# Loads of an overflow branch on GpSimd's queue in place of ScalarE's, with a larger descriptor scratch and one buffer for small values

## The chip, the cores and the metric

The kernel runs on one core of one Trainium2 chip. The core has TensorE (PE: matrix products and transposes), VectorE (DVE), ScalarE (ACT) and GpSimd (POOL) for elementwise work, SyncE (SP), which here only issues transfers, and 16 DMA engines that move data between HBM and the on-chip memory. Each engine works through its own list of instructions; they meet at semaphores. The metric is the device time of one execution in microseconds.

## The reference

The reference computes two layers on 256 tokens of width 1024, and a final RMSNorm. A layer has a mixer with three parallel groups of heads, and a hierarchical mixture of experts. All is float32. The part that matters here, shortened:

```python
def hier_moe(h, w_group, b_group, w_expert, b_expert, w_gate, w_up, w_down):
    t = h.reshape(B * S, D)                      # 256 x 1024
    g_prob = softmax(t @ w_group + b_group)      # 4 groups
    p_sel, g_idx = top_k(g_prob, 1)
    e_in = logits of the 8 experts of that group
    w_k, i_k = top_k(softmax(e_in), 2)           # 2 of 8, weights normalised
    combine = p_sel * one_hot(g_idx) * inner     # 256 x 4 x 8
    for g in range(4):
        a, b = t @ w_gate[g], t @ w_up[g]        # 8 experts of 1024 x 256
        hid = silu(a) * b * combine[:, g]
        y += hid @ w_down[g]                     # 8 experts of 256 x 1024
```

All 32 experts of a layer are read, 3 MB each, so a layer has about 100 MB of expert weights.

## The kernel before

**Staging.** Weights come from HBM into a ring of 25 slots of 1 MB each (128 partitions x 2048 floats), which also holds most intermediate values. A rehearsal of the program notes when each slot is free; from it the place of each load in SyncE's list is set. All weight loads (line 80) go through SyncE's queue, in the order in which they are used. They count on eight semaphores in turn, DMAHW0 to DMAHW7, and a load waits for the load eight before it, so that at most eight are under way. Where a slot was in use, the load also waits for the engine that used it last.

**A layer.** The mixers come first (lines 413 to 637), then the routing (640), then the experts (799). Four experts form a group; there are eight groups. For each expert at most 32 tokens (CAP) are gathered into slots by a matrix product with a 0/1 matrix (`collect`). `hidden` multiplies them with 8 MB of gate and up weights per group, `bend` and `turn` apply the gate and transpose, and for groups 0 to 3 `whole` multiplies with 4 MB of down weights and adds to x. For groups 4 to 7 the down products are put off into four rounds at the end (line 901), between which the input projection of the next layer is done.

**The overflow branch.** If an expert has more than 32 tokens, the surplus is dropped by the gathering and must be added. After group 1 the largest count of a layer is put into `flag` (line 893). After group 3, `overflow` (line 940) has each of the five engines read the flag (line 951) and compare it (line 952). The branch takes five slots of the ring, which it shares with the weights:

```python
        count = nc.values_load(flag[0:1, 0:1], min_val=0, max_val=S)
        with self.tc.If(count > CAP):
            ...
            with self.tc.For_i(0, 96, 12) as e0:
                for j in range(4):
                    for k in range(8):
                        nc.scalar.dma_start((g0, g1)[k // 4][:, k % 4 * 512:k % 4 * 512 + 512],
```

The body computes the surplus for all experts, one expert at a time, with 12 loads of 256 KB for each. In the kernel before they are issued by ScalarE's queue, which counts on the same eight semaphores as SyncE's loads. When an engine doesn't take the branch, it runs a short block in which the semaphores that the body would have raised are raised by as much; in the profile this block has line 952.

**Small values.** Values of a few bytes per partition (`ss`, `s`, `r1`, `rr`, `low`, `sums`, `cm`, `flag`, `ws` and the like) lie in the pool `sm`, where a name has two buffers by default. The names of `route` ask for one buffer themselves. SCRATCH, 512 bytes per partition, is set aside for transfer descriptors that GpSimd writes.

Of the kernel before, what the change touches and what calls it, by code (L numbers as in the profile page):

```python
# [9 lines left out]
F32 = mybir.dt.float32  # L10
# [13 lines left out]
AHEAD = 3  # L24
NV = 61
TAIL = 4
SCRATCH = 512
SM_UK, SM_UV, SM_PW, SM_RT = 0, 512, 1024, 1280


# [87 lines left out]
def v3(t, a, b, c0=0):  # L118
    return t[:, c0:c0 + a * b].rearrange("p (a b) -> p a b", a=a)


class Net:
    def __init__(self, tc, ctx, a, plan):
        self.tc, self.nc, self.a, self.plan = tc, tc.nc, a, plan
        nc = self.nc
        into = ctx.enter_context if plan else lambda c: c
        big = into(tc.tile_pool(name="big", bufs=1))
        cst = into(tc.tile_pool(name="cst", bufs=1))
        self.sm = into(tc.tile_pool(name="sm", bufs=2))
        psp = into(tc.tile_pool(name="ps", bufs=1, space=bass.MemoryType.PSUM))  # L130
        into(tc.manual_schedule())
        self.ps = psp.tile([128, 8, 512], F32, name="ps")
# [57 lines left out]
        g = nc.gpsimd  # L190
# [12 lines left out]
        for i, n in ((0, 4), (8, 32)):  # L203
            k = min(i, 4)
# [18 lines left out]
    def mm(self, out, lhsT, rhs, start, stop):  # L223
        self.nc.tensor.matmul(out, lhsT, rhs, start=start, stop=stop, skip_group_check=True)  # L224
# [574 lines left out]
    def experts(self, l, routed):  # L799
        nc, ps, ring, vec, sm, mm = self.nc, self.ps, self.ring, self.vec, self.sm, self.mm  # L800
        V, A, G = nc.vector, nc.scalar, nc.gpsimd
        r2, comb, pos, sel, st = routed
# [23 lines left out]

        def bend(g, dT):

            d, h, ws = st[g][0], st[g][2][:, 0:256], sm.tile([128, 1], F32, name="ws")
            A.activation(h, ps[:, 2, 0:256], AF.Silu)  # L830
            for t in range(2):
                self.tr(ps[:, 3, 256 + t * 128:256 + t * 128 + 128], d[:, t])
            V.tensor_reduce(ws, ps[:, 3, 256:512], axis=AX.X, op=OP.add)  # L833
            V.scalar_tensor_tensor(h, h, ws, ps[:, 2, 256:512], op0=OP.mult, op1=OP.mult)  # L834
            V.tensor_scalar(dT, ps[:, 3, 256:512], 0.0, None, op0=OP.is_gt)  # L835
# [31 lines left out]
        for g in range(8):  # L867
            if g == 8 - TAIL:
                th, tw = ring.take("th"), ring.take("tail", F32R)
            hidden(g)  # L870
            i = (g - 8 + TAIL) * 512
            hT, dT = (st[g][1][:, j:j + 2].rearrange("p k s -> p (k s)") for j in (0, 2)) if i < 0 else (
                th[:, i // 2:i // 2 + 256], tw[:, i // 2:i // 2 + 256])
            bend(g, dT)
            if g == 0:
                hv = v3(ring.take("hn"), 2, D)
                for t in range(2):
                    self.ev("a", hv[:, t], self.x[:, t], r2[:, t:t + 1])
            if g + 1 < 8:
                collect(g + 1)  # L880
            turn(g, hT)
            if i < 0:
                whole(g, hT, dT)
            else:
                tail[g] = hT, dT
                ring.drop(f"g{g}")
            if g == 1:

                cm, flag = sm.tile([128, 1], F32, name="cm"), sm.tile([128, 1], I32, name="flag")
                for t in range(2):  # L890
                    mm(ps[:, 3, 0:32], self.ones, sel[:, t], t == 0, t == 1)
                V.tensor_reduce(cm, ps[:, 3, 0:32], axis=AX.X, op=OP.max)
                V.tensor_copy(flag, cm)
            if g == 3:
                self.overflow(l, hv, comb, pos, flag)
# [44 lines left out]
    def overflow(self, l, hv, comb, pos, flag):  # L940

        nc, ps, ring, mm = self.nc, self.ps, self.ring, self.mm
        V, A, we = nc.vector, nc.scalar, self.a["we"]
        names = ("ohT", "og0", "og1", "od", "om")
        hT, g0, g1, dn, om = (ring.take(n) for n in names)
        if not self.plan:
            return ring.drop(*names)
        hx, cw = v3(hT, 8, 256), v3(om, 2, 32)
        wd = dn.rearrange("p (q c n) -> p q c n", q=4, c=2)
        hd, fT, tmp = v3(om, 2, 256, 64), v3(om, 2, 256, 576), v3(om, 2, 32, 1088)  # L950
        count = nc.values_load(flag[0:1, 0:1], min_val=0, max_val=S)
        with self.tc.If(count > CAP):
            V.tensor_scalar(cw, pos, CAP - 0.5, None, op0=OP.is_ge)
            V.tensor_tensor(cw, cw, comb, op=OP.mult)
            for k in range(8):
                for t in range(2):
                    self.tr(ps[:, k % 2, t * 128:t * 128 + 128], hv[:, t, k * 128:k * 128 + 128])
                self.ev("av"[k % 2], hx[:, k], ps[:, k % 2, 0:256], self.vec[:, l, 8 + k:9 + k])
            with self.tc.For_i(0, 96, 12) as e0:
                for j in range(4):  # L960
                    for k in range(8):
                        nc.scalar.dma_start((g0, g1)[k // 4][:, k % 4 * 512:k % 4 * 512 + 512],
                                            we[bass.ds(e0 + (l * 96 + k), 1), :, j * 512:j * 512 + 512]
                                            .rearrange("o p c -> (o p) c"))
                    for q in range(4):
                        nc.scalar.dma_start(dn[:, q * 512:q * 512 + 512],
                                          we[bass.ds(e0 + (l * 96 + 8 + q), 1), :, j * 512:j * 512 + 512]
                                          .rearrange("o p c -> (o p) c"))
                    for t in range(2):
                        for k in range(8):  # L970
                            mm(ps[:, t], hx[:, k, t * 128:t * 128 + 128], v3((g0, g1)[k // 4], 4, 512)[:, k % 4],
                               k == 0, k == 7)
                        A.activation(hd[:, t], ps[:, t, 0:256], AF.Silu)
                        V.scalar_tensor_tensor(hd[:, t], hd[:, t], cw[:, t, j:j + 1], ps[:, t, 256:512],
                                               op0=OP.mult, op1=OP.mult)
                        for c in range(2):
                            self.tr(ps[:, 3, c * 256 + t * 128:c * 256 + t * 128 + 128],
                                    hd[:, t, c * 128:c * 128 + 128])
                    V.tensor_copy(fT, v3(ps[:, 3], 2, 256))
                    for t in range(2):  # L980
                        for n in range(2):
                            for c in range(2):
                                mm(ps[:, 4 + 2 * t + n], fT[:, c, t * 128:t * 128 + 128],
                                   wd[:, 2 * n:2 * n + 2, c], c == 0, c == 1)
                            xs = self.x[:, t, n * 512:n * 512 + 512]
                            V.tensor_tensor(xs, xs, ps[:, 4 + 2 * t + n], op=OP.add)
                V.tensor_copy(tmp[:, :, 0:28], cw[:, :, 4:32])
                V.tensor_copy(cw[:, :, 0:28], tmp[:, :, 0:28])
        ring.drop(*names)
# [112 lines left out]
```

## Time and profile before

| | |
|---|---|
| median of 3 runs | 608.64 us (606.15 to 609.34) |
| the profiled execution | 607.07 us |
| its span, first to last instruction | 605.4 us |
| mean granted TensorE clock | 0.951 |
| PE busy | 530.0 us (88%) |
| DVE busy | 261.3 us (43%) |
| ACT busy | 142.4 us (24%) |
| POOL busy | 96.5 us (16%) |
| transferred | 228.67 MB, mean 378 GB/s |
| loads on SyncE's queue | 92.6% of the DMA engines' time |

Busy shares are averages over stages with different limits: TensorE is busy for most of the span, and so are the DMA engines. Which of them ends a stage is read from the waits in that stage. The page's rate row divides the span into 40 slices of 15.1 us. In it the experts of layer 0 run from about slice 9 to slice 22 and those of layer 1 from about slice 29 to the end; between them lies the mixer of layer 1. The names are those of the program: `slot` is a slot of the ring, `in_we` the expert weights, `ps` the accumulators. An engine's name with a q (SPq, POOLq) is its sequencer, where branches, semaphores and transfer issues run.

### The profile page before, as it was taken

How to read it: one execution, taken by the hardware profiler on the slowest of the kernel's cores; microseconds unless marked ns; L12 is line 12 of the kernel's file. 1: busy time of each engine (PE TensorE's matmuls, PEld its weight loads, DVE VectorE, ACT ScalarE, POOL GpSimd, SP SyncE). 2: the span in 40 equal slices, each digit the busy share in tenths (PEclk: the TensorE clock that was granted, in tenths of full speed). 3: DMA queues.
4: the chain of work that ended last, by engine and by line, in shares of the span. 5: the costliest groups of instructions: out<-in, count | busy, mean ns of one | idle time of the engine just before them, and what ended most of it. 6: DMA issues, size and time to landing. Idle time of an engine off the chain costs nothing. (4 is left out here: it accounts for less than half of the span.)

```text
span 605.4 us, 10375 instructions
## 1 busy us (share of the span) xinstructions
PE 530.0 (88%) x4168; PEld 335.9 (55%) x4168; DVE 261.3 (43%) x644; ACT 142.4 (24%) x339; POOL 96.5 (16%) x138
## 2 busy tenths in 40 slices
PE   8989999898898687779989899998898878886993
PEld 8959877554344143426768787765344425431662
DVE  5879765332333122115357876652333322221242
ACT  4476453200000000013234854322000000001222
POOL 2544322000000000002113442310000000000011
PEclk9999999999999799859999999998999997996897
DMA  8999878999999979999999959689999998999993
GB/s 309 399 421 397 331 254 326 368 391 424 421 420 420 416 292 422 423 418 419 421 420 422 422 206 333 261 334 395 422 420 421 420 419 368 372 421 422 422 410 107
DMA packets 34618, 228.67 MB, mean 378 GB/s; under 512 B 3841, under 2 KB 6145, under 8 KB 7938
## 3 DMA queue, kind: packets, MB, share of 16 engines
q1 hardware_dynamic: 34130, 227.33, 92.6%
q8 instruction: 36, 0.59, 0.4%
q10 hardware_dynamic: 432, 0.59, 0.3%
q14 instruction: 20, 0.16, 0.1%
HBM read 226.85 MB, written 1.05 MB: 376 GB/s over the span
## 5 line engine op out<-in xcount | busy, mean ns | idle before, releaser
L224 PE MATMUL ps<-slot,slot 128*32 128x256 f32 (+6 forms) x3372 | 410.1, 440 | 56.5 <-DVE slot L780 23.2
L224 PEld LDWEIGHTS ps<-slot,slot 128*32 128x32 f32 (+2 forms) x3372 | 245.6, 144 | 190.2 <-issue 91.7
L242 POOL TENSOR_TENSOR slot<-slot,slot 128x512 fp32r<-128x512 f32 (+1 forms) x38 | 50.9, 1339 | 131.0 <-DVE slot L290 53.0
L288 ACT ACTIVATE slot<-ps 128x256 fp32r<-128x256 f32 (+5 forms) x70 | 33.1, 473 | 142.8 <-PE ps L224 129.0
L833 DVE TENSOR_REDUCE ws<-ps 128x1 f32<-128x256 f32 x16 | 6.8, 424 | 133.1 <-PE ps L282 133.1
L224 PE MATMUL ps<-slot 128*128 128x256 f32 (+3 forms) x224 | 59.2, 408 | 0.0
L830 ACT ACTIVATE slot<-ps 128x256 f32<-128x256 f32 x16 | 6.1, 383 | 215.8 <-PE ps L224 215.8
L809 POOL TENSOR_TENSOR slot<-slot,comb 128x128 f32<-128x128 f32 x32 | 12.1, 399 | 270.0 <-PE ps L224 215.9
L242 DVE TENSOR_TENSOR slot<-slot,slot 128x512 fp32r<-128x512 f32 (+1 forms) x54 | 47.5, 881 | 13.5 <-ACT slot L288 13.1
L224 PEld LDWEIGHTS ps<-slot 128*128 128x128 f32 (+1 forms) x224 | 30.5, 195 | 30.9 <-issue 14.4
L793 DVE TENSOR_TENSOR slot<-ps,vec 128x512 f32<-128x512 f32 x32 | 22.1, 691 | 52.5 <-PE ps L224 52.3
L290 DVE COPY slot<-ps 128x512 f32<-128x512 f32 (+3 forms) x30 | 20.5, 689 | 40.9 <-PE ps L224 32.6
L242 DVE TENSOR_TENSOR slot<-ps,slot 128x256 fp32r<-128x256 f32 (+1 forms) x42 | 18.3, 435 | 43.8 <-ACT slot L288 43.7
L288 ACT ACTIVATE slot<-slot 128x512 fp32r<-128x512 f32 (+1 forms) x54 | 33.0, 613 | 15.4 <-PE ps L224 10.9
L282 PE MATMUL ps<-ident,slot 128*128 128x128 f32 x128 | 24.3, 295 | 5.0 <-DVE slot L835 2.9
L282 PEld LDWEIGHTS ps<-ident,slot 128*128 128x128 f32 x128 | 14.8, 145 | 24.3 <-issue 15.4
L863 DVE TENSOR_TENSOR x<-x,ps 128x512 f32<-128x512 f32 x32 | 22.0, 688 | 8.5 <-PE ps L224 8.2
L224 PE MATMUL ps<-ident,ones 128*128 128x128 f32 x108 | 19.2, 314 | 1.5 <-POOL ident L193 1.5
L244 DVE SCALAR_TENSOR_TENSOR slot<-ps,vec,slot 128x256 fp32r<-128x256 f32 x26 | 12.4, 482 | 17.8 <-ACT slot L288 17.7
L288 ACT ACTIVATE slot<-ps,vec 128x256 fp32r<-128x256 f32 x26 | 12.1, 473 | 27.6 <-PE ps L282 13.2
L290 DVE CAST slot<-slot 128x512 fp32r<-128x512 f32 (+1 forms) x38 | 18.5, 487 | 0.0
L224 PEld LDWEIGHTS ps<-ident,ones 128*128 128x128 f32 x108 | 16.1, 218 | 3.9 <-issue 2.4
(126 smaller groups left out, 303.2 us busy)
## 6 DMA issues: line engine op xcount, KB each, us to landing
slot<-in_we SPq DMA_DIRECT2D x191, 1024.0 KB, 19.2
slot<-in_wo SPq DMA_DIRECT2D x8, 1024.0 KB, 19.2
slot<-in_wvu SPq DMA_DIRECT2D x4, 1024.0 KB, 19.8
slot<-in_wqk SPq DMA_DIRECT2D x3, 1024.0 KB, 19.3
slot<-in_wa SPq DMA_DIRECT2D x3, 832.0 KB, 14.1
slot<-in_uq SPq DMA_DIRECT2D x2, 1024.0 KB, 15.5
slot<-in_small SPq DMA_DIRECT2D x2, 784.0 KB, 15.7
x<-in_x SPq DMA_DIRECT2D x4, 256.0 KB, 5.8
```

The lines of the kernel that those rows point to most:

```text
L224: self.nc.tensor.matmul(out, lhsT, rhs, start=start, stop=stop, skip_group_check=True)
L242: V.tensor_tensor(lo, in_, hi.bitcast(F32), op=OP.subtract)
L244: V.scalar_tensor_tensor(lo, in_, scale, hi.bitcast(F32), op0=OP.mult, op1=OP.subtract)
L282: self.nc.tensor.transpose(out, in_, self.ident)
L288: nc.scalar.activation(out, in_, AF.Copy, scale=1.0 if scale is None else scale)
L290: nc.vector.tensor_copy(out, in_)
L793: self.nc.vector.tensor_tensor(xs[:, 4 * n:4 * n + 4], v3(self.ps[:, b0 + n], 4, 128), self.vec[:, l, 8 + 4 * n:12 + 4 * n, None].to_broad ...
L809: G.tensor_tensor(d4, d4, comb[:, t, 4 * g:4 * g + 4, None].to_broadcast([128, 4, 32]), op=OP.mult)
L830: A.activation(h, ps[:, 2, 0:256], AF.Silu)
L833: V.tensor_reduce(ws, ps[:, 3, 256:512], axis=AX.X, op=OP.add)
L863: V.tensor_tensor(xs, xs, ps[:, 6 + n], op=OP.add)
```

## The change

The twelve loads in the body of the branch are issued by GpSimd in place of ScalarE. GpSimd's loads count on eight semaphores of their own, DMASW0 to DMASW7. The scratch for descriptors goes from 512 to 1,024 bytes. The pool `sm` has one buffer per name, and only `ws` keeps two.

```diff
-SCRATCH = 512
+SCRATCH = 1024
...
-        self.sm = into(tc.tile_pool(name="sm", bufs=2))
+        self.sm = into(tc.tile_pool(name="sm", bufs=1))
...
-            d, h, ws = st[g][0], st[g][2][:, 0:256], sm.tile([128, 1], F32, name="ws")
+            d, h, ws = st[g][0], st[g][2][:, 0:256], sm.tile([128, 1], F32, name="ws", bufs=2)
...
-                        nc.scalar.dma_start((g0, g1)[k // 4][:, k % 4 * 512:k % 4 * 512 + 512],
+                        nc.gpsimd.dma_start((g0, g1)[k // 4][:, k % 4 * 512:k % 4 * 512 + 512],
                                             we[bass.ds(e0 + (l * 96 + k), 1), :, j * 512:j * 512 + 512]
...
-                        nc.scalar.dma_start(dn[:, q * 512:q * 512 + 512],
+                        nc.gpsimd.dma_start(dn[:, q * 512:q * 512 + 512],
```

On SyncE, at the end of the branch in layer 0, the program before has the following. The row of line 952 stands for the block of the branch that isn't taken, with what it waits for; the rows of line 80 are the first weight loads behind it, by the slot that they fill.

```order
L952 UNCONDITIONAL_BRANCH [waits DMAHW0_49,DMAHW1_49,DMAHW2_49,DMAHW3_49,DMAHW4_49,DMAHW5_49,DMAHW6_49,DMAHW7_49]
L80 DMA slot_1895<-in_we 128x2048 [waits DVE_49,DMAHW1_49,PE_49,Activation_49]
L80 DMA slot_1897<-in_we 128x2048 [waits DMAHW6_49,DMAHW5_49,DMAHW7_49,DMAHW2_49,DMAHW0_49]
L80 DMA slot_1899<-in_we 128x2048 [waits DMAHW4_49,DMAHW3_49]
L80 DMA slot_1907<-in_we 128x2048 [waits PE_49]
L80 DMA slot_1913<-in_we 128x2048 [waits DMAHW5_49,PE_49]
```

The changed program has the following at the same place.

```order
L952 UNCONDITIONAL_BRANCH
L80 DMA slot_1895<-in_we 128x2048 [waits DVE_49,DMAHW1_49,PE_49,Activation_49]
L80 DMA slot_1897<-in_we 128x2048 [waits DMASW7_49,DMASW6_49,DMAHW2_49,DMASW5_49,DMASW4_49]
L80 DMA slot_1899<-in_we 128x2048 [waits DMASW3_49,DMASW2_49,DMAHW3_49,DMASW1_49,DMASW0_49]
L80 DMA slot_1907<-in_we 128x2048 [waits DMAHW4_49,PE_49]
L80 DMA slot_1913<-in_we 128x2048 [waits DMAHW5_49,PE_49]
```

The eight waits of line 952 are gone from SyncE, and the second and third load wait for semaphores of GpSimd's transfers.

On GpSimd, at the end of the same branch, the difference between the two programs is this; lines 959 are the end of the loop in the body, line 952 the block of the branch not taken, and line 809 the weighting of group 5's gathering matrix.

```order
 L959 REGISTER_ALU
 L959 COMPARE_AND_BRANCH
 L959 UNCONDITIONAL_BRANCH
+L952 ISA
 L952 UNCONDITIONAL_BRANCH
 L809 TENSOR_TENSOR slot_1956<-slot_1956,comb 128x128 x2
```

GpSimd has one more instruction in the block not taken, which raises DMASW0 to DMASW7. The body of the loop ahead of it holds the loads that stood on ScalarE before. TensorE's, VectorE's and SyncE's rows are otherwise the same.

## Rows read from the trace of the kernel before

**Rows 1.** The page, rate of transfers in 40 slices of the span
```profile
GB/s 309 399 421 397 331 254 326 368 391 424 421 420 420 416 292 422 423 418 419 421 420 422 422 206 333 261 334 395 422 420 421 420 419 368 372 421 422 422 410 107
```

**Rows 2.** The chain that ended last, layer 1's experts: start us, us, what
```profile
518.22 14.32 DMA slot<-in_we
...
532.60 20.54 DMA slot<-in_we
...
557.87 38.33 PE ps L224 x384
```

**Rows 3.** Waits of SyncE's queue, whole span: us, times, longest us
```profile
SPq L80 <- DMA slot<-in_we: 195.1, 97, 3.0
...
SPq L952 <- SPq L952: 37.2, 6, 18.5
```

**Rows 4.** Line 952: durations in ns, then first and last start us
```profile
L952 SPq EVENT_SEMAPHORE  x16: 17/17/17, 220.1 to 514.6; - x16
L952 POOLq COMPARE_BRANCH  x2: 45/45/45, 190.1 to 483.9; - x2
...
L952 SPq COMPARE_BRANCH  x2: 45/49/53, 201.6 to 495.6; - x2
```

**Rows 5.** Timeline, load issues of SyncE around both branches: start us, us
```profile
178.00 22.69 SPq L80 DMA_DIRECT2D slot<-in_we  x10
...
221.17 7.13 SPq L80 DMA_DIRECT2D slot<-in_we  x9
...
227.98 0.33 SPq L80 DMA_DIRECT2D slot<-in_we  x1
...
494.61 0.33 SPq L80 DMA_DIRECT2D slot<-in_we  x1
...
514.79 5.74 SPq L80 DMA_DIRECT2D slot<-in_we  x9
...
520.20 0.33 SPq L80 DMA_DIRECT2D slot<-in_we  x1
```

**Rows 6.** Windows: busy us of each engine, then PEclk, DMA share, GB/s
```profile
180.00:195.00 15.00, 12.47 (x138) 7.21 (x130) 4.01 (x9) 0.98 (x2) 0.76 (x2) 1.00 1.01 419
217.50:227.50 10.00, 9.17 (x83) 3.73 (x81) 2.33 (x5) 0.38 (x1) 0.76 (x2) 1.00 0.63 220
510.00:517.50 7.50, 7.50 (x60) 4.82 (x63) 1.81 (x3) 0.00 (x0) 0.76 (x2) 0.83 0.59 214
```

**Rows 7.** Timeline, TensorE behind the branch of layer 0 (idle before, releaser)
```profile
204.44 8.73 PE L224 MATMUL ps<-slot,slot 128*32 128x512 f32 x57 [4.73 <-issue]
```

**Rows 8.** TensorE's waits from 228 to 300 us, and its timeline there
```profile
PE ps L224 <- DMA slot<-in_we: 7.2, 8, 1.4
...
237.85 1.06 PE L224 MATMUL ps<-slot,slot 128*32 128x512 f32 x8 [0.21 <-DMA slot<-in_we]
...
277.61 0.64 PE L224 MATMUL ps<-slot,slot 128*32 128x256 f32 x8 [0.26 <-DMA slot<-in_we]
```

**Rows 9.** Layer 1's end: TensorE's waits (540 to 556), timeline, windows
```profile
PE ps L224 <- DMA slot<-in_we: 5.3, 5, 1.5
...
553.18 1.94 PE L224 MATMUL ps<-slot,slot 128*32 128x512 f32 x8 [0.55 <-DMA slot<-in_we]
...
593.64 1.07 PE L224 MATMUL ps<-slot,slot 128*32 128x256 f32 x16
...
550.00:555.00 5.00, 3.75 (x16) 0.40 (x16) 0.00 (x0) 0.00 (x0) 0.00 (x0) 0.50 1.01 419
590.00:592.50 2.50, 2.50 (x36) 1.42 (x26) 0.73 (x2) 0.39 (x1) 0.00 (x0) 1.00 0.79 254
592.50:595.00 2.50, 2.50 (x31) 1.76 (x28) 0.42 (x1) 0.60 (x2) 0.00 (x0) 1.00 0.02 8
```

**Rows 10.** GpSimd: the instruction's kind at the start, and behind the branch
```profile
L1095 POOLq INC_SWDGE_SEM  x1: 27/27/27, 0.2 to 0.2; - x1
...
218.94 0.76 POOL L809 TENSOR_TENSOR slot<-slot,comb 128x128 f32<-128x128 f32 x2 [28.83 <-PE ps L224]
```

## The prediction, made before the changed kernel had run

> **What bounds the kernel now.** I read the page's rate row first: the transfers run at about 420 GB/s through both expert stages, and in each stage there is one hole, where the rate falls to 292 and then to 368 and 372 [rows 1]. So there the weight stream is the resource to look at, and the question is what opens the two holes. The chain of waits comes next: from 518 to 553 us it is almost all weight transfer, and from 557.87 us it is TensorE without another transfer in it [rows 2]. The expert stage of layer 1 therefore ends when its weights land, and the tail behind it follows at TensorE's own pace. Third, the waits of SyncE's queue. Most of them are the normal ones, a load waiting for the load eight before it (195.1 us over 97 waits), but 37.2 us sit on line 952, the overflow branch, one of them 18.5 us long [rows 3]. The rows of that line show what it is: SyncE compares and branches at 201.6 and 495.6 us, and then runs 16 semaphore instructions, 8 per branch, of which the first ends at 220.1 and the last at 514.6 us [rows 4]. The overflow body itself never runs: its loads, line 962, have no row in the trace.
>
> Why SyncE waits there can be read in the program. The scalar engine's loads of the overflow body count on the same eight semaphores (DMAHW0 to 7) as SyncE's weight loads. A branch that isn't taken has to bring these semaphores to where the body would have left them, and SyncE does it: for each it waits until all earlier loads on it have landed, then adds. SyncE thus lets the weight queue run empty at each of the two branches.
>
> **What an emptied queue costs.** Before the first branch ten loads are issued in 22.69 us, 0.33 us of which is the last issue itself: (22.69 - 0.33) / 9 = 2.484 us a load of 1 MB [rows 5]. The last of them goes out at 200.36 us. After the drain nine loads are issued from 221.17 on, and the ninth, at 227.98 us, is the first that again waits for a landing [rows 5]. Nine loads at the old pace would have brought it at 200.36 + 9 x 2.484 = 222.72 us. The drain of layer 0 cost 5.26 us. The same in layer 1: 494.61 + 22.36 = 516.97 against 520.20 us, 3.23 us [rows 5]. By bytes, as a second way: from 217.5 to 227.5 us 220 GB/s were moved where 419 had been usual, (419 - 220) x 10 / 419 = 4.75 us; from 510 to 517.5 us 214, which is 3.67 us [rows 6]. The two ways sum to 8.49 and 8.42 us; I take 8.45, with 7.98 (4.75 + 3.23) and 8.93 (5.26 + 3.67) as ends.
>
> **The change part by part.**
>
> The loads of the body go to GpSimd's queue, and so to semaphores of their own (DMASW0 to 7). In the order of the changed kernel SyncE's branch row has no waits any more, and GpSimd has one instruction and the waits on its own semaphores instead. The first load behind the branch waits for the landing that any load waits for, and for TensorE, VectorE and ScalarE to have passed the branch. It would be due at 200.36 + 2.48 = 202.84 us. SyncE is through the comparison at 201.7 us [rows 4], so it issues on time. Its slots are free: the first three held down-projection weights of group 3, which TensorE is done with before its own branch, and the next ones gate and up weights of group 4; of these TensorE needs 57 multiplications in 8.73 us from 204.44 us on, 8 to a weight [rows 7], so it frees one every 1.2 us, twice as fast as loads come. So both holes close: minus 8.45 us on the transfers' side.
>
> How much of it reaches the end. Layer 0: TensorE begins to starve at 237.85 us and has its last wait for a weight, of 0.26 us, at 277.61 us [rows 8]; behind that it is bound by itself until the mixers are through. The arrival at 277.61 moves with the loads. Can TensorE be there 5.26 us earlier? It loses 7.2 us in 8 waits on the way [rows 8], more than 5.26, so it would still have some 2 us of waiting left: the loads stay the later ones, and the whole 5.26 (or 4.75) passes on. Layer 1 then runs the same course, only earlier. There the last gate and up weight is waited for at 553.18 us, and 5.3 us in 5 waits in all [rows 9], again more than the loads gain; the chain from there is TensorE's, and the 3.23 to 3.67 us pass on too. The last weights land near 592.3 us (254 GB/s until 592.5, 8 after), and are used at 593.64 [rows 9], so the tail has 1.3 us of room and isn't caught by them, since both move alike.
>
> What GpSimd pays. It now runs an instruction that raises the eight semaphores at the branch not taken. Its kind is in the trace once, at the start, with 27 ns [rows 10]; below it isn't worth anything, and above I bound it by the longest stop that an engine shows behind this branch, TensorE's 4.73 us [rows 7]. I take 27 ns. Either way it is hidden: GpSimd takes its branch at 190.1 us [rows 4] and sits idle for 28.83 us before its next work, at 218.94 [rows 10]. Without that cover each microsecond would delay the weighting of group 5. SyncE's second load waits for these semaphores too; it is due at 205.3 us, 15 us after.
>
> TensorE stands still for 4.73 us behind its branch and "issue" is all that the profile names [rows 7]. The Trainium skill (Runtime: NRT & Kernel Launch, Instruction fetch mechanics) says that a taken branch to code outside the fetched window waits until that code has been fetched. By this rule SyncE, whose wait at the branch has so far covered such a fetch, may be held likewise: 201.7 + 4.73 = 206.4 us for its next load, two loads late with six still under way, so the sum stays, but the rule gives rival 3 its chance. No row of SyncE can show it before the change.
>
> ScalarE loses the 96 loads of the two bodies and as many address instructions, none of which ran: 0. The scratch is touched by no instruction that runs: 0. One buffer for small values makes a second layer's value wait for the first's readers; the nearest case is the flag, read for layer 0 before SyncE's comparison at 201.6 us [rows 4] and written again only in the experts of layer 1, behind a whole mixer: 0. A few later instructions wait for more semaphores than before, all raised at the branch; each costs some 17 ns [rows 4], under 0.3 us in all.
>
> **The sum.** 607.07 us of the profiled execution (605.4 span and 1.7 around it) minus 8.45 is 598.6. That execution is 1.6 us below the median of the runs, from which the same sum gives 600.2. I predict the middle, 599.4 us.
>
> **The rivals.**
>
> 1. The clock gives more. From 550 to 555 us the granted clock is 0.50, the lower of the two levels (1.2 GHz), and a step of 8 multiplications takes 1.94 us instead of 1.06 [rows 8, 9], behind the waits for weights. With fewer starved loads this may not come. TensorE could then gain some 2 us until 560, but the last weights allow only the 1.3 us of room: 598.1 us. Against it: starving doesn't vanish, it only begins later, and the same fall could come elsewhere, for as much the other way.
>
> 2. Only one hole pays, or a hole is worth less. If TensorE turned out to be the later one at 277.61, where it waits only 0.26 us, layer 0's gain would be lost and 3.45 us remain: 604.4 us. Against it stand the 7.2 us of waits before. Beside it, the Trainium skill (DMA: Bandwidth & Descriptors, Anatomy of one DMA) gives a transfer from GpSimd's path a fixed cost of about 2.0 us whatever its size. Were that all that an emptied queue loses, two would be 4.0 us and the time 603.9; the trace disagrees, with 4.75 and 3.67 us.
>
> 3. It doesn't do what it says: SyncE is held behind the branch until the queue is empty all the same, by a fetch or by another engine's semaphore. It would have to be held for 18 us, and the longest stop seen is 4.73 [rows 7]. Time 607.9 us.
>
> 4. Slower: the semaphores that SyncE's second load waits for are now raised by GpSimd. They decide once GpSimd raises them later than that load goes out now, after 221.7 us, 31.6 us after its branch; from there each microsecond costs one, in both layers. At 34 us that is about 2 x 2.4, some 613 us. For it: the instruction isn't timed in this use. Against it: 27 ns in the one use that there is [rows 10].
>
> **Chances.** The forecast 0.74, with a range of its own of 597 to 602 us (the ends of the sum, 0.95 us apart, the 1.6 us between median and profiled run, and some 2 us of clock either way); rival 1 0.12; rival 2 0.07; rival 3 0.04; rival 4 0.03. A range of 595.5 to 604.0 holds the forecast, rival 1 and part of rival 2. Half a percent, 3 us, is about what a measurement of this kernel tells from no change. Faster by more: 0.92 (the forecast, rival 1 and most of rival 2); within: 0.05; slower: 0.03.
>
> **What would show it.** Right: line 952 has no long wait on SyncE, and loads follow at about 2.48 us across 200 and 490 us; the rate row has no hole in either expert stage; TensorE's starving starts some 5 us later than 237.85 or is shorter by as much; layer 1's flag read comes about 5 us earlier and the end about 8. A stop of SyncE behind the branch with the transfers still at 419 GB/s would bear out the fetch, at no cost. Wrong: a hole of the same depth with a wait on GpSimd's semaphores (rival 4) or with none (rival 3); or closed holes and a TensorE that reaches 277 us no earlier (rival 2).

## The result, and the profile after

The changed kernel takes 602.16 us (median, 601.02 to 603.37), the kernel before 608.94: 6.8 us less, a ratio of 0.9898 with an interval of 0.9867 to 0.993. Forecast were 599.4 us with a range of 595.5 to 604.0. The profiled execution took 601.43 us (span 599.8). The mechanism is the one foretold, and the gain is smaller than its sum of 8.45 us: the time lies inside the wide range, and just above the range of 597 to 602 us that the forecast had for itself.

The rate row of the page after, against [rows 1]:

```profile
GB/s 300 402 419 413 294 281 306 368 389 423 420 420 422 414 422 422 418 423 417 422 419 421 412 200 325 273 325 392 415 423 421 419 419 421 419 422 423 420 398 89
```

Both holes are gone: slice 15 stands at 422, where 292 was, slices 34 and 35 at 421 and 419, where 368 and 372 were. The windows that had 220 and 214 GB/s [rows 6] now read (last column GB/s, before it PEclk and DMA share):

```profile
217.50:227.50 10.00, 9.82 (x88) 4.38 (x87) 1.86 (x4) 0.38 (x1) 0.76 (x2) 1.00 1.02 420
510.00:517.50 7.50, 7.38 (x67) 2.11 (x66) 0.93 (x3) 0.39 (x1) 0.40 (x2) 1.00 1.02 421
```

The waits of SyncE's queue after (us in all, times, longest us), against [rows 3]:

```profile
SPq L80 <- DMA slot<-in_we: 233.0, 117, 3.6
SPq L80 <- PE ps L224: 142.1, 68, 17.6
```

The 37.2 us on line 952 have no row any more; what SyncE waits for is the landing eight loads back, 117 times instead of 97. The rows of line 952 after (ns min/median/max, first and last start), against [rows 4, 10]:

```profile
L952 POOLq EVENT_SEMAPHORE  x8: 17/43/43, 191.2 to 486.2; - x8
L952 POOLq COMPARE_BRANCH  x2: 45/45/45, 190.7 to 480.7; - x2
...
L952 POOLq INC_SWDGE_SEM  x2: 157/167/177, 196.2 to 486.3; - x2
...
L952 SPq COMPARE_BRANCH  x2: 50/52/53, 202.4 to 492.4; - x2
```

SyncE has its comparison and nothing else. GpSimd has the new instruction instead, 157 to 177 ns long and not 27, and in layer 0 it starts 5.5 us behind the comparison. Its next work comes at 219.59 us, after 28.87 us of idling, so none of this is paid:

```profile
219.59 0.76 POOL L809 TENSOR_TENSOR slot<-slot,comb 128x128 f32<-128x128 f32 x2 [28.87 <-PE ps L224]
```

Single loads of SyncE around both branches, from its timeline (start us, us), against [rows 5]:

```profile
201.13 0.33 SPq L80 DMA_DIRECT2D slot<-in_we  x1
203.63 0.33 SPq L80 DMA_DIRECT2D slot<-in_we  x1
...
223.47 0.33 SPq L80 DMA_DIRECT2D slot<-in_we  x1
227.49 0.33 SPq L80 DMA_DIRECT2D slot<-in_we  x1
...
327.83 0.33 SPq L80 DMA_DIRECT2D slot<-in_we  x1
...
491.42 0.33 SPq L80 DMA_DIRECT2D slot<-in_we  x1
493.90 0.33 SPq L80 DMA_DIRECT2D slot<-in_we  x1
...
513.92 0.33 SPq L80 DMA_DIRECT2D slot<-in_we  x1
517.75 0.33 SPq L80 DMA_DIRECT2D slot<-in_we  x1
...
569.83 2.43 SPq L80 DMA_DIRECT2D slot<-in_we  x1
```

The branch lies between the first two, and they are 2.50 us apart; nine loads later SyncE is at 223.47 us, 22.34 behind 201.13, which is nine times 2.48. But the tenth load follows only after 4.02 us, and in layer 1 after 3.83. There the rate doesn't fall, and SyncE waited for nothing but a landing. These two gaps were not foreseen.

TensorE after, against [rows 7 to 9]: the stop behind the branch is still there, starving begins at 249.92 us (237.85 before), and the last wait of layer 1 has moved from 553.18 to 547.53 us, with the same fall of its step to 1.94 us:

```profile
204.70 9.12 PE L224 MATMUL ps<-slot,slot 128*32 128x512 f32 x59 [4.26 <-issue]
...
249.92 1.06 PE L224 MATMUL ps<-slot,slot 128*32 128x512 f32 x8 [0.27 <-DMA slot<-in_we]
...
547.53 1.94 PE L224 MATMUL ps<-slot,slot 128*32 128x512 f32 x8 [1.41 <-DMA slot<-in_we]
```

It still loses 4.9 us in 5 waits for weights from 225 to 300 us, and 4.6 us in 4 from 530 to 556:

```profile
PE ps L224 <- DMA slot<-in_we: 4.9, 5, 1.4
...
PE ps L224 <- DMA slot<-in_we: 4.6, 4, 1.4
```

One of these waits is the same in both kernels, before the first row and after the second. In the changed kernel it is the last one of layer 0; the wait at 277.61 us [rows 8] is gone.

```profile
267.50 1.94 PE L224 MATMUL ps<-slot,slot 128*32 128x256 f32 x16 [0.46 <-DMA slot<-in_we]
...
264.28 1.93 PE L224 MATMUL ps<-slot,slot 128*32 128x256 f32 x16 [0.46 <-DMA slot<-in_we]
```

**Where the 5.5 us of the two profiled executions lie.** The changed kernel is 0.77 us later at the last load before the first branch (201.13 against 200.36), which no part of the change explains. From that load to the 51st behind it (327.83 against 331.24) it gains 4.16 us. In layer 1, from the last load before the branch to the 32nd behind it, it gains 2.59 us: these are the loads at 491.42 and 569.83, and before at 494.61 and 575.62. The two later loads of the kernel before, which stand in no group yet:

```profile
331.24 0.33 SPq L80 DMA_DIRECT2D slot<-in_we  x1
...
575.62 2.43 SPq L80 DMA_DIRECT2D slot<-in_we  x1
```

At the very end it loses 0.6 us. One execution of each is not enough for parts of this size, so the same stretches were read in every later profile:

```
us, from the last load before the branch        layer 0              layer 1         SyncE's last issue
                                          to 9th   to 51st     to 9th   to 32nd      to end
before                                     27.61   130.87       25.59    81.01        5.00
e2 other edits alone                       25.79   130.06       26.79    82.48        4.99
e3 body on SyncE's queue                   27.81   130.92       25.38    81.38        5.00
e7 before, small body                      25.46   129.54       25.26    80.93        5.29
e4 GpSimd in layer 0 only                  23.17   126.72       25.63    81.25        5.04
e9 GpSimd in layer 1 only                  25.80   130.11       22.59    78.39        5.04
after                                      22.34   126.71       22.50    78.42        5.61
e11 after, again                           22.34   126.70       22.34    77.96        5.61
e1 queue change alone                      22.34   126.72       22.57    78.53        5.61
e6 after, small body                       22.35   126.83       22.41    77.92        5.43
e8 after, side loads                       22.40   126.79       22.45    78.89        5.60
e5 no branch                               22.34   126.75       22.35    78.48        4.65
e10 no branch, again                       22.47   126.62       22.36    76.94        4.65
```

Each number is the difference of two issue times in one trace. Where the queue drains in layer 0 (five kernels), 130.30 us in the mean to the 51st load; where it doesn't (six, with a branch), 126.74: 3.56 us. In layer 1: 81.41 (five) against 78.24 (five, e8 left out): 3.17 us.

### The profile page after: what moved, and what is told of

Read it like the earlier page. It is cut to its first block, busy times and chain, and to the rows that moved or that the text cites. A ratio compares the mean times of both kernels' runs of the same rounds, so it can differ in the third digit from the quotient of the medians.

```text
span 599.8 us, 10395 instructions
## 1 busy us (share of the span) xinstructions
PE 526.3 (88%) x4168; PEld 332.7 (55%) x4168; DVE 261.2 (44%) x644; ACT 142.7 (24%) x339; POOL 96.6 (16%) x138
## 5 line engine op out<-in xcount | busy, mean ns | idle before, releaser
L224 PEld LDWEIGHTS ps<-slot,slot 128*32 128x32 f32 (+2 forms) x3372 | 242.8, 143 | 187.2 <-issue 94.6
```

## The experiments

The theory from the prediction is called A: semaphores that the body's loads share with SyncE's weight loads make the queue drain, and each drain costs some microseconds. Its rivals B to D, and the two theories on the new gaps (H and S), are told with the runs that tell them apart.

**e1: the queue alone.** The move of the body's loads, with scratch 512 and two buffers for small values.

```
 SCRATCH = 512
 sm = tile_pool(name="sm", bufs=2)
-nc.scalar.dma_start(...)      # both loads of the overflow body
+nc.gpsimd.dma_start(...)
```

> The move of the body's loads to GpSimd's queue alone; scratch 512, two buffers for small values as before. Theory A (the semaphores that SyncE's weight loads shared with the body's loads made the queue drain, and nothing else in the change matters): no long wait of SyncE on line 952, no hole in the rate row, 602.2 us like the changed kernel, within 1 us. Rival B (part of the gain comes from the single buffer or the scratch): 604 to 607 us.

602.13 us, ratio to the kernel before 0.9898 (0.9871 to 0.9925), the same as the whole change, and the same stretches. The queue is the whole effect.

**e2: the other edits alone.**

```
+SCRATCH = 1024; sm bufs=1; ws bufs=2
 nc.scalar.dma_start(...)      # unchanged
```

> The other edits alone: scratch 1,024, one buffer for small values and two for ws, the body's loads still on ScalarE's queue. Theory A: 8 semaphore instructions of SyncE per branch and both holes as before, 608.9 us, within 1 us. Rival B: 603 to 607 us.

609.81 us against 609.15, ratio 1.0006 (0.9981 to 1.0032). SyncE's 16 semaphore instructions are back:

```profile
L952 SPq EVENT_SEMAPHORE  x16: 17/17/17, 221.6 to 516.0; - x16
```

Rival B falls with these two.

**e3: the body on SyncE's own queue.**

```
-nc.gpsimd.dma_start(...)
+nc.sync.dma_start(...)
```

> The changed kernel with the body's loads on SyncE's own queue. Theory A: they count on SyncE's semaphores again, so the block of the branch not taken waits for all eight; both holes and 18 us waits on line 952 return, 608 to 610 us. Rival C (it was ScalarE's queue, as another queue beside SyncE's, that cost time): no holes, 602 us.

608.81 us, ratio 0.9996 (0.997 to 1.0023), and in the trace:

```profile
L952 SPq EVENT_SEMAPHORE  x16: 17/17/17, 223.6 to 518.8; - x16
```

and among the waits of SyncE's queue:

```profile
SPq L952 <- SPq L952: 38.5, 6, 19.5
```

ScalarE's queue is not used by the body here, and the drain is as long as before. So another queue beside SyncE's is not needed for the drain; loads that count on SyncE's semaphores are enough. A body on ScalarE's queue with semaphores of its own, which would part queue and semaphores altogether, was not built. Rival C falls.

**e4 and e9: one layer each.**

```
-nc.gpsimd.dma_start(...)
+(nc.gpsimd, nc.scalar)[l].dma_start(...)      # e4; e9: (nc.scalar, nc.gpsimd)[l]
```

> The changed kernel with GpSimd's queue in layer 0 only; layer 1 keeps ScalarE's. The profile after gives layer 0 a gain of 3.95 us at the arrival that ended at 277.61 us before, and layer 1 one of 2.46 us. Theory A with these sizes: 608.9 - 3.95 = 605.0 us, the hole of layer 1 as deep as before (20 us between two loads). By the prediction's sizes 608.9 - 5.26 = 603.7 us. Rival D (only one of the two holes pays, and it is the one of layer 1): 608.9 us.

> The changed kernel with GpSimd's queue in layer 1 only, the counterpart of the kernel with layer 0 only. The stages of the profiles so far give layer 1 a gain of 3.2 us (86.5 against 83.2 us from load 193 to load 227) and layer 0 one of 3.6. If the two add: 608.9 - 3.2 = 605.7 us, layer 0 from load 86 to 138 in 132 to 133.4 us. If the layers don't add (one hides the other): 608.9 or 602.2 us.

e4: 604.85 us, 0.9927 (0.9906 to 0.9949), so 4.4 us for layer 0 with 3.1 to 5.7. e9: 605.68 us, 0.9944 (0.9924 to 0.9965), so 3.4 us for layer 1 with 2.1 to 4.6. Each pays, and they add within their intervals. The rate row of e4 has the second hole alone (slices 34 and 35), that of e9, below it, the first (slice 15):

```profile
GB/s 300 401 419 406 286 274 303 367 394 422 419 421 420 415 422 419 420 421 420 421 420 422 391 199 329 245 348 392 425 420 420 421 417 360 381 423 422 422 408 103
```

```profile
GB/s 284 402 418 414 295 274 307 368 392 424 420 421 420 416 306 427 421 420 421 419 419 423 420 140 349 305 324 365 421 421 420 419 421 418 420 420 421 422 411 111
```

Rival D falls.

**e5 and e10: no branch.** The slots are taken and given back; the overflow of tokens above the capacity is left out.

```
-        if not self.plan:
+        if True:
             return ring.drop(*names)
```

> The changed kernel without the overflow branch: the slots of the body are taken and given back, but no comparison, no branch and no body are there, so tokens above the capacity are left out. Theory H (the two gaps that the changed kernel still has, 4.02 us after 223.47 and 3.83 us after 513.92 where loads follow at 2.48, come from instruction packets on the DMA engines: at the branch they bunch, 3 of 16 KB within 12 us instead of one in 13 to 25, each holds up one of the 16 engines by over 1 us, and a load has landed only with its slowest engine): packets at their usual spacing, TensorE's stop of 4.3 us gone, no gap over 3 us behind 200 or 490 us, 599 to 601 us. Rival S (these loads, or their slots, are late in any version): both gaps stay, 601.5 to 602.5 us.

> The kernel without the overflow branch once more, beside the changed kernel. In its first profile both expert stages took as long as in the changed kernel (129.11 against 129.18, 83.45 against 83.35 us), and its 3 us less came from the mixers and the two ends. Theory N (the mixers' part is chance, 1.6 us each): within 1 us of the changed kernel beside it, 600.5 to 602 us. Theory B (the branch itself still costs): 3 us below the changed kernel, 599 us, with the expert stages as before.

> The changed kernel itself, beside the kernel without a branch: 602.2 us; loads 86 to 138 in 129.2 us and 193 to 227 in 83.3 us, with one gap of 3 to 4 us in each, where a 16 KB instruction packet starts.

e5: 598.91 us, 0.986 (0.9825 to 0.9895). Run again, beside the changed kernel (e11), it took 600.82 us (e10), 0.9876 (0.9845 to 0.9907), and the changed kernel 602.43, 0.9887 (0.9858 to 0.9917). The intervals overlap, so theories N and B stay undecided; in the stretches of layer 0 there is nothing (126.75 and 126.62 against 126.74), in layer 1 they disagree (78.48 and 76.94 against 78.24), and about 1 us lies behind SyncE's last issue (4.65 against 5.61). The gaps, however, settled a question of their own. Theory H expected none over 3 us. e5 has one of 4.02 us all the same, the same size as in the changed kernel, only at another load (single loads of SyncE):

```profile
262.38 0.33 SPq L80 DMA_DIRECT2D slot<-in_wa  x1
266.40 0.33 SPq L80 DMA_DIRECT2D slot<-in_we  x1
```

So the gap isn't made by packets that bunch at the branch, against H, nor does it belong to certain loads, against rival S. What is left of H, the instruction packets themselves, is taken up under the gaps below.

**e6 and e7: a shorter body.** The four experts of a step as an inner loop, on GpSimd's queue (e6) and on ScalarE's (e7).

```
-                for j in range(4):
+                with self.tc.For_i(0, 2048, 512) as j0:
...
-            we[..., j * 512:j * 512 + 512]
+            we[..., bass.ds(j0, 512)]
```

> The changed kernel with the body's four experts of a step as an inner loop: TensorE's instructions between the branch and what follows it fall from some 160 to some 95. Theory H, if packets are fetched by the distance that is jumped: a shorter stop than 4.3 us, fewer packets behind the branch, one gap or none, 600 to 601.5 us. If they are fetched at every taken branch whatever its length: as the changed kernel, 602.2 us. Rival S: 602.2 us.

> The kernel before (loads of the body on ScalarE's queue, scratch and buffers as in the changed kernel) with the same inner loop. Theory A: SyncE still waits for all eight semaphores, both holes stay; a packet that falls into a hole costs nothing, so a shorter jump gains little, 608 to 609 us. If the hole's depth comes from the fetch and not from the semaphores: 605 us or less.

e6: 602.53 us, 0.9904 (0.9873 to 0.9934). TensorE's stop behind the branch is gone (compare the 4.26 above):

```profile
200.19 7.07 PE L224 MATMUL ps<-slot,slot 128*32 128x512 f32 x64 [0.15 <-PEq L952]
```

and the time is that of the changed kernel. So the stop of 4.3 us costs nothing: TensorE waits for weights a little later anyhow. e7: 607.99 us, 0.9999 (0.9977 to 1.002), with both drains, as theory A has it. The body's length neither makes nor fills the holes.

**e8: side loads.** A direct attempt to hold up one DMA engine.

```
+            if l == 1 and 3 <= g < 7:
+                for i in range(8):
+                    nc.gpsimd.dma_start(<one row of band>, <one row of we, 2,560 bytes>)
```

> The changed kernel with 32 extra loads of one row each (2,560 bytes, one packet, 0.15 us on one DMA engine) on GpSimd's queue, 8 in each of groups 3 to 6 of layer 1, into a constant that is no longer read. Theory L (a load lands with the slowest of the 16 engines, so a packet costs all loads its own time when it falls on that engine, and nothing when it falls on another): if the rows fall on one engine, 32 x 0.15 = 4.8 us of hold-up less a lead of about 2 us, so loads 193 to 227 take 85 to 88 us instead of 83.35, in gaps behind the rows, and the time is 604 to 607 us; spread over the engines, 0.3 us. Rival W (engines share the work, so only bytes count): 82 KB at 420 GB/s, 0.2 us, 602.4 us.

603.6 us, 0.9909 (0.9876 to 0.9941). The rows did not stay whole: the trace has 1,024 packets of the new queue for 32 loads, the data in pieces of 160 bytes, so they spread over the engines. Layer 1's stretch took 78.89 us, some 0.5 above the changed kernel's, which neither theory excludes. This run tells nothing apart.

## What the gaps are

The trace has 16 raises of a semaphore for each load, and 16 packets of 4 bytes in each 2.48 us: one for each of the 16 DMA engines, which end their shares of a load one by one. The load has landed with the last of them. From the changed kernel, in rows of 2.48 us, the time of one load: where the row starts in us, and how long after it each of these packets started. The trace doesn't name a packet's engine; it is known here by its place in the row. The first of a row is the last to end a load, the others are already some way into the next:

```
218.00  0.00 0.33 0.43 0.48 0.83 1.27 1.59 1.66 1.91 1.92 1.98 2.00 2.05 2.05 2.27 2.28
220.48  0.01 0.33 0.43 0.49 0.83 1.27 1.60 1.67 1.91 1.92 1.99 2.01 2.05 2.05 2.27 2.29
222.95  0.02 0.34 0.44 0.49 0.84 1.29      1.67 1.91 1.91 1.92 1.99 2.01 2.05 2.05 2.27 2.28
225.43       0.34 0.43 0.49 0.83 1.29 1.56 1.67 1.91 1.92 1.99 2.02 2.05 2.06 2.27 2.29 2.33
```

Row by row every engine keeps its place, 2.48 us later each time, until one is missing: the first of the third row, due again at 225.45, came at 226.99 us (1.56 in the fourth row), 1.54 late. Of the others, the one at 1.60 came 0.3 us late in the third row and later still in the fourth; the rest kept their places. The late first engine is the one for which SyncE waits: each load of this stretch is issued 0.5 us after its packet (222.97 and 223.47, 226.99 and 227.49). The semaphore says the same: fifteen of its 16 raises had come by 225.88 us, the last came at 227.43. What came in between is an instruction packet; in the window from 224 to 225 us the trace has one of 16 KB and one of 8 (packets, MB, share):

```profile
q8 instruction: 1, 0.02, 6.9%
q14 instruction: 1, 0.01, 1.9%
```

The larger starts at 224.22 us and takes 1.10 us. There are 36 such packets in the whole execution (32 to 36 in the 13 profiles), and they come whatever the kernel does at the branch. Taking all 13 profiles together, the stretches of the table, without the drains themselves, have 28 gaps of over 2.9 us between two loads. 27 of them start within 1.4 us of the start of a 16 KB packet; by chance some 4 would. By this reading a packet that falls on an engine which is ahead costs nothing, and one on the slowest engine shows as a gap, 0.4 to 1.7 us over the usual 2.48. It rests on coincidence in time and on the tracks above, and is not shown: e8, which was to force it, told nothing apart, and another was not tried.

The Trainium skill (Runtime: NRT & Kernel Launch, Instruction fetch mechanics) says that engines fetch code ahead in 16 KiB blocks by a DMA queue of their own, and that crossing a block is mostly hidden. The packets are there, of that size. For the weight stream they are not hidden, if the reading above is right: the tracked load landed 1.54 us late.

## Why the prediction was right, and where its size was off

**The mechanism: right.** Line 952 has no wait of SyncE, loads follow at 2.5 us across both branches, the holes are closed; e1 and e2 show that the queue change is all of the effect, and e3 that the drain goes with the shared semaphores.

**Passing on to the end: right.** TensorE kept 4.9 and 4.6 us of waits for weights, so it stayed the earlier one, and the gains of both layers arrive; e4 and e9 show each alone in the total. The wait that both kernels have comes 3.22 us earlier (264.28 against 267.50), although the changed kernel was 0.77 us later at the branch: 3.99 of the loads' 4.16 us. The signs were off with the size: SyncE's comparison in layer 1 came 3.2 us earlier (492.4 against 495.6) instead of about 5, and TensorE's starving began 12 us later instead of 5.

**GpSimd's instruction: the duration was wrong, the cost right.** 157 to 177 ns instead of 27, and 5.5 us from comparison to instruction, more than the 4.73 that served as a bound; the idle 28.9 us hide it. SyncE's second load, which waits for it, went out at 203.63 us, 7 us after it: rival 4 was never near. SyncE was held by no fetch, so rival 3 has nothing for it either.

**The other edits and ScalarE's loads: 0, right** (e2: 1.0006).

**Layer 1, forecast 3.23 to 3.67 us: right in size,** if a little high: 2.59 in the two profiles, 3.17 in the mean of five against five.

**Layer 0, forecast 5.26 by issue pace and 4.75 by bytes: this is the step that failed.** It measured 3.56 us. Two things were taken for the drain that were not. First, one profile stood for all. The nine loads that took 27.61 us in the kernel before (5.25 more than nine at 2.484) took 25.46 to 25.80 in three of the other four kernels that drain there, so 3.1 to 3.4 us; the mean of the five is 26.49, 4.13 us. In the two deeper ones the first load behind the drain, for whose landing the ninth waits, took 6.7 us (before) and 6.2 (e3) from issue to landing, in the other three 4.9 (the first row is of the kernel before, the second of e2):

```profile
slot<-in_we SPq DMA_DIRECT2D x1, 1024.0 KB, 6.7
...
slot<-in_we SPq DMA_DIRECT2D x1, 1024.0 KB, 4.9
```

What delayed it is not settled. In the kernel before the second load after the drain took SyncE itself 1.24 us instead of 0.33,

```profile
221.69 1.24 SPq L80 DMA_DIRECT2D slot<-in_we  x1
```

and an instruction packet of 16 KB began at 221.15 us, as the first one went out. In e3 the third load took 2.21 us, with such a packet from 225.47 us on. But e9 has a packet at nearly the same place and lost only 3.4 us. Second, the price was taken against a stream that keeps 2.484 us for good. It doesn't: in every kernel without a drain the stretch to the 51st load holds about 1.5 us of hold-ups like the gaps above (loads that are smaller than 1 MB give as much back, which is why 126.7 is 51 x 2.484). Of the 4.13 us that the drain had cost at the ninth load, 3.56 are left at the 51st: kernels that drain lose less afterwards. The table has it by kernel: from the ninth to the 51st load the two deeper ones take 103.26 and 103.11 us, the three others 104.08 to 104.31, and those with a branch and without a drain 104.36 to 104.48 (e4, with a hold-up ahead of its ninth load, 103.55). What a drain has lost early is not lost again, as if the hold-ups fell into the hole, where they cost nothing. That last reading is argued, not tested.

**The sum.** Forecast 8.45 us. Measured by stretches 3.56 + 3.17 = 6.73, less 0.6 at the end: 6.1. By medians 6.8, with an interval of 4.3 to 8.1 us. The 0.6 us was not in the working: the last store on ScalarE's queue lands 3.3 us after its issue instead of 2.7 (KB, us to landing; after, then before),

```profile
out<-slot ACTq DMA_DIRECT2D x1, 256.0 KB, 3.3
```

```profile
out<-slot ACTq DMA_DIRECT2D x1, 256.0 KB, 2.7
```

and in the changed kernel an 8 KB instruction packet starts at 596.9 us, beside it. The four profiles with such a packet beside this store (the changed kernel twice, e1 and e8) land it after 3.3 us and end 5.6 us behind SyncE's last issue; all others land it after 2.7 and end after 5.04 or less, but for e6 and e7, the short bodies, with 5.43 and 5.29, which stay unexplained. That the packet delays the store is again a coincidence in time.

The forecast's own range of 597 to 602 us allowed 0.95 us for the size of the drains. That was too little, and the time lies just above it; the wide range held it because it reached into rival 2, a hole that is worth less.

**The rivals.** Rival 1: the clock fell at the same place as before, and the step there takes the same 1.94 us. But the kernel before had the lower clock once more in the tail, from 570.5 to 573.9 us (granted 0.50), and the changed one did not (the same step, before and after):

```profile
571.28 1.94 PE L224 MATMUL ps<-slot,slot 128*32 128x256 f32 x16
...
566.38 1.07 PE L224 MATMUL ps<-slot,slot 128*32 128x256 f32 x16
```

At 555 us it went the other way, one step of the changed kernel (at 555.16) taking 1.94 us instead of 1.07 (before, at 560.59). TensorE's lead in this pair, read from ScalarE's matching rows, goes from 5.65 us (before 555.18) to 4.56 (561.73) and 6.11 (575.75), so the clock gave about 0.5 us. A second stretch like that near 570 us is also in e4, which drains in layer 1, and in e8, which doesn't. Rival 2 said that a hole may be worth less, which came true in part, by another way than its own: TensorE at 277 us took nothing from the gain. The 2.0 us that the Trainium skill (DMA: Bandwidth & Descriptors, Anatomy of one DMA) gives a transfer of GpSimd's path as its fixed cost is no measure for an emptied queue; the runs have 3.56 and 3.17.

## What to carry to other kernels

A branch that is never taken can still stop a queue: if its body's DMAs count on the semaphores of a running stream, the other side of the branch first waits for that stream to land. Give the body a queue with semaphores of its own; here that was worth 3.4 us a branch. When a stall is priced from one profile, take the price at the end of the stage and from more than one execution: right behind the hole it was 4.13 us here, at the end of the stage 3.56, and single drains of layer 0 ranged from 3.1 to 5.5 us at the ninth load.

## What the runs showed of the hardware

- An instruction packet of 16 KB takes 1.07 us (median of 36 in the changed kernel), where a data packet of 8 KB takes 0.31. Where one falls beside a full weight stream a load can land 0.4 to 1.7 us late, with no dip in the rate row and no other wait to be seen. That the packet is the cause rests on 27 of 28 gaps that coincide.
- TensorE stopped for 4.26 and 4.50 us, a few multiplications behind the branch, where the body was long, and for 0.15 us in both layers where it was short (e6); two lengths don't show what decides. The Trainium skill (Runtime: NRT & Kernel Launch, Instruction fetch mechanics) says that a target outside the fetched window must be fetched first; that would fit, but no run here shows the window.
- The instruction that raises GpSimd's DMA semaphores took 157 to 177 ns at the branch and 27 ns at the start of the program.
- A load of one row of 2,560 bytes from GpSimd's queue was cut into 16 packets of 160 bytes (e8), where SyncE's load of one 4 KB row (`fg`) went as a single packet; what decides this is not shown.
